# Another set of seven-product weight groups in a two-layer decoder trunk, with an accumulating transfer for one weight sum and the query and key squares summed on ScalarE

## The chip, the cores and the metric

The program runs on one core of one Trainium2 chip. The metric is the device time of one execution, in microseconds (us); the kernel before takes 1815.41 us (median of 3 runs, 1814.85 to 1815.59). The engines are named as in the profile: PE is TensorE, DVE VectorE, ACT ScalarE, POOL GpSimd and SP SyncE. On this chip each engine works through its own instructions in order; an instruction that waits holds up all that stand behind it on the same engine. PEld are PE's loads of a stationary operand, which run beside its matmuls.

## What is computed

Two layers are applied to x of 512 tokens by 2048 features. Each normalises x, projects it with one weight matrix, runs three mixers on slices of the projection, gates each, and projects the 2048 mixed features back into the residual:

```python
def _layer(x, norm_g, w_in, conv_w, conv_b, sb_qn_g, sb_kn_g, gla_w_up, gla_b_up, gla_on_g, w_out):
    h = _rmsnorm(x, norm_g)
    proj = h @ w_in                                   # 2048 x 7696
    (cv_h, cv_b, cv_c, cv_g, sb_q, sb_k, sb_v, sb_g, gl_q, gl_k, gl_v, gl_g, gl_lr) = split(proj)
    y_conv = _short_conv(cv_h, cv_b, cv_c, conv_w, conv_b) * silu(cv_g)
    q, k = _rmsnorm(sb_q, sb_qn_g), _rmsnorm(sb_k, sb_kn_g)      # 8 heads of 128
    y_sb = _stick_breaking(q, k, sb_v) * silu(sb_g)
    g = log_sigmoid(gl_lr @ gla_w_up + gla_b_up) / 16
    o = _gla(gl_q, gl_k, gl_v, g)                     # 4 heads, keys of 64, values of 128, decayed
    y_gla = _rmsnorm(o, gla_on_g) * silu(gl_g)
    return x + concat(y_conv, y_sb, y_gla) @ w_out
```

## The kernel before

**Weight groups.** The weights are worked through in groups of 256 columns by 2048 rows, 38 a layer, always in the order of the list `specs`: two value groups of the gated linear attention (GLA), its query, its key, its two gates, four groups of the first half of the convolution (h, c, g, b), then for each of four pairs of heads of the attention v, g, q, k (v 0, g 0, q 0, k 0, v 1, ...), the four groups of the second half of the convolution, and eight groups of the output projection. `fetch` loads a group's 2 MB on SP's queue two groups ahead, into one of two buffers `st`. `load_` prepares it one group ahead: `wmax` (ACT, squares with their sum), an all-reduce on POOL and a few instructions on 128x1 columns on DVE (`wscale`) give a power of two, and the scaled weights are split into two f16 parts, the high one by ACT and the low one by DVE. The inputs are split in the same way, so that a product takes three f16 matmuls (high by high, high by low, low by high).

**Plain and seven-product groups.** A plain group is split in two halves (lines L432 on ACT, L439 on DVE) and multiplied by 16 k-tiles in `project_cols` (features on the partitions, 96 matmuls of 512 columns) or `project_toks` (tokens on the partitions, 192 of 256 columns). A group named in `QUICK_IN` or `QUICK` is taken as a 2x2 block matrix and multiplied with seven block products instead of eight, by a scheme of the Strassen kind (`project_quick`: 168 matmuls of 256 columns, or 336 of 128). Before it, `wsums` forms sums of the four weight blocks b11, b12, b21, b22 with four DVE additions in place in `st` and splits seven blocks (L471 on ACT, L472 on DVE) into seven operands; after it, DVE and ACT combine the products. The products also need four sums of the blocks of the input: the first, fifth and seventh product read the input alone, the second and sixth read one of the four sums each, and so do the third and the fourth. `xsums` makes them once a layer: 24 additions of 128x1024 on DVE (one line, L673) and 8 copies on ACT (L681). Its scratch tiles come from the tags `zw` and `g`, of which there are two buffers each.

**What sets the order.** Beyond a part at the very start that is ordered by hand, a scheduler places the instructions of every engine when the program is built, by dependencies, by free buffers and by its own estimate of the times; the order on each engine is then fixed. Code written later comes later in it only where dependencies, priorities or buffers make it so. The weights' preparation has a higher priority. The squares of the next group are issued after the instruction in `lasthi`.

**Around the change.** `xsums()` is called ahead of the GLA's query. The GLA works on two pairs of heads (p = 0, 1). For each, seven levels of block products are built (L998 to L1012: differences on DVE, Exp on ACT, splits on ACT and DVE, `mm3` on PE, a masked copy into the tile `attd`, of the tag `zw`, on DVE), then four inter-chunk products (L1059, L1060), then the products with the values (L1072). The tail of each pair, for each of two heads, scales the result (L1078), squares it on ACT, means it on PE (L1082), takes Ln and Exp on ACT, and runs six DVE instructions of 128x512 (L1086 to L1091). In the attention, v is split (L1241, L1242) and its largest size found by DVE and an all-reduce (L1243, L179); queries and keys are squared by ACT in two halves of 128x512 (L1271), summed by DVE in groups of 128 (L1272), normalised, split, transposed by DMA and used for scores (L1181) a group or two later.

## Time and profile before

| | |
|---|---|
| median of 3 runs | 1815.41 us |
| the profiled execution | 1812.69 us, of which the span is 1810.9 us |
| mean granted clock of PE | 0.973 |
| PE, PEld busy | 1687.5 us (93%), 1384.3 us (76%) |
| DVE busy | 1447.8 us (80%) |
| ACT busy | 1149.2 us (63%) |
| POOL busy | 75.7 us (4%) |
| stretch from the GLA's query to the attention's first query, layer 1 and 2 | 269.2 us, 270.4 us |
| stretch of the attention and the second convolution half, layer 1 and 2 | 409.8 us, 408.2 us |
| output projections | 162.8 us, 161.2 us |

A row of a group of instructions reads: line, engine, operation, tile written <- tiles read, shape, count, then busy time in us and mean ns of one, then the engine's idle time ahead of these instructions and what ended it. A row of a table of windows gives a stretch (start and end in us from the start of the span), its length, and each engine's busy time in it with the number of instructions; PEclk is the granted clock of PE. Busy times of matmuls hold their drain, so the distance between two starts is less than a matmul's duration.

### The profile page before, as it was taken

The numbers are of one execution on the slowest core, as the hardware profiler recorded it, in microseconds if no ns is written. First come the engines' busy times: TensorE is split into PE (matmuls) and PEld (weight loads), VectorE is DVE, ScalarE is ACT, GpSimd is POOL, SyncE is SP. The second block draws the span as 40 slices with busy tenths as digits, with TensorE's granted clock in tenths as the row PEclk, the third lists the DMA queues.
The fourth block names the chain that finished last, engine by engine and source line by source line (L and its number), as shares of the span: only waits on it lengthen the run. The fifth ranks groups of instructions, "written<-read, shape, count | busy, mean of one in ns | idle before, by whom it ended". The sixth has DMA issues, their size and how long they took to land. (4 is left out here: it accounts for less than half of the span.)

```text
span 1810.9 us, 37130 instructions
## 1 busy us (share of the span) xinstructions
PE 1687.5 (93%) x15786; PEld 1384.3 (76%) x15786; DVE 1447.8 (80%) x2539; ACT 1149.2 (63%) x1459; POOL 75.7 (4%) x106
## 2 busy tenths in 40 slices
PE   8997979889998999999999878889899989999999
PEld 6656756778887885689986666568888888847998
DVE  8989997768687786777598899976687868767884
ACT  7568766746574665656666686755575657655562
POOL 1100000000000000000011000000000000000000
PEclk9998989999999999999999999999999999999999
DMA  6221222333554447344643112314253635562541
GB/s 238 94 93 48 94 90 69 115 114 109 143 127 121 113 128 217 108 147 151 213 117 125 48 52 95 99 59 152 71 169 83 175 77 160 163 189 76 180 143 48
DMA packets 297926, 217.83 MB, mean 120 GB/s; under 512 B 118482, under 2 KB 296988, under 8 KB 297248
## 3 DMA queue, kind: packets, MB, share of 16 engines
q1 hardware_dynamic: 288752, 206.01, 38.2%
q10 hardware_dynamic: 9008, 9.45, 1.5%
q8 instruction: 123, 2.02, 0.4%
q14 instruction: 43, 0.35, 0.1%
HBM read 179.65 MB, written 14.68 MB: 107 GB/s over the span
## 5 line engine op out<-in xcount | busy, mean ns | idle before, releaser
L653 PE MATMUL psp<-wh,m 128*128 128x256 f16 x1088 | 296.4, 273 | 2.9 <-DVE v L1242 1.8
L655 PE MATMUL psp<-wh,m 128*128 128x256 f16 x1088 | 296.5, 273 | 0.0
L654 PE MATMUL psp<-wl,m 128*128 128x256 f16 x1088 | 296.5, 273 | 0.0
L472 DVE SCALAR_TENSOR_TENSOR wl<-st,ws,wh 128x1024 f16<-128x1024 f32 x186 | 235.0, 1279 | 71.4 <-ACT wh L471 71.1
L365 ACT ACTIVATE junk<-st 128x2048 uint8<-128x2048 f32 x150 | 285.0, 1900 | 4.4 <-DMA st<-in_w_out_dram 2.9
L471 ACT ACTIVATE wh<-st,ws 128x1024 f16<-128x1024 f32 x186 | 205.8, 1140 | 88.6 <-PE psp L655 33.5
L732 PE MATMUL psp<-s,wh 128*128 128x256 f16 x1280 | 229.8, 280 | 27.5 <-ACT wh L471 8.2
L439 DVE SCALAR_TENSOR_TENSOR wl<-st,ws,wh 128x2048 f16<-128x2048 f32 x90 | 211.1, 2348 | 54.2 <-ACT wh L432 53.6
L432 ACT ACTIVATE wh<-st,ws 128x2048 f16<-128x2048 f32 x88 | 175.5, 1998 | 93.3 <-DVE wp L395 31.2
L732 PEld LDWEIGHTS <-wh 128*128 128x128 f16 x1920 | 193.2, 101 | 47.4 <-ACT wh L471 15.5
L732 PE MATMUL psp<-s,wl 128*128 128x256 f16 x640 | 178.8, 280 | 4.9 <-DVE wl L472 4.3
L653 PE MATMUL psp<-wh,x 128*128 128x256 f16 x640 | 174.3, 273 | 2.9 <-DVE v L1242 1.9
L654 PE MATMUL psp<-wl,x 128*128 128x256 f16 x640 | 174.4, 273 | 0.0
L655 PE MATMUL psp<-wh,x 128*128 128x256 f16 x640 | 174.4, 273 | 0.0
L732 PEld LDWEIGHTS <-wl 128*128 128x128 f16 x960 | 96.6, 101 | 59.8 <-issue 26.9
L654 PEld LDWEIGHTS <-m 128*128 128x128 f16 x1088 | 106.5, 98 | 14.6 <-issue 2.4
L653 PEld LDWEIGHTS <-m 128*128 128x128 f16 x1088 | 106.5, 98 | 13.2 <-issue 0.6
L655 PEld LDWEIGHTS <-m 128*128 128x128 f16 x1088 | 106.5, 98 | 12.5 <-issue 0.2
L378 POOL PARTITION_ALL_REDUCE wgm<-wm x75 | 46.1, 615 | 1537.1 <-ACT junk L365 1316.0
L779 PEld LDWEIGHTS <-m 128*128 128x128 f16 x768 | 74.8, 98 | 13.5 <-DMA m<-raw 3.1
L645 PE MATMUL psp<-x,wh 128*128 128x512 f16 x192 | 74.0, 385 | 9.8 <-ACT wh L432 9.8
L645 PEld LDWEIGHTS <-wh 128*128 128x128 f16 x384 | 37.9, 99 | 56.0 <-ACT wh L432 12.5
(426 smaller groups left out, 3833.6 us busy)
## 6 DMA issues: line engine op xcount, KB each, us to landing
st<-in_w_in_dram SPq DMA_DIRECT2D x120, 1024.0 KB, 7.6
st<-in_w_out_dram SPq DMA_DIRECT2D x32, 1024.0 KB, 6.7
mixd<-ga SPq DMA_DIRECT2D x24, 256.0 KB, 2.6
x<-in_x_dram SPq DMA_DIRECT2D x4, 1024.0 KB, 4.9
qT<-in_x_dram ACTq DMA_DIRECT2D x8, 512.0 KB, 4.7
qT<-xs ACTq DMA_DIRECT2D x8, 512.0 KB, 3.8
xs<-x SPq DMA_DIRECT2D x14, 256.0 KB, 4.8
out_dram<-kT SPq DMA_DIRECT2D x14, 256.0 KB, 2.8
```

Source lines behind the costliest of these rows:

```text
L365: S.activation(junk(HK * GW).rearrange("p (k n) -> p k n", k=HK), staged[i][h], AF.Square, accum_out=peak[i][:, h:h + 1])
L378: G.partition_all_reduce(gm, peak.pop(i), P, RED.add)
L432: lasthi[i] = S.activation(wh[:, :, :GW], staged[i][h], AF.Copy, scale=scales[i])
L439: V.scalar_tensor_tensor(wl[:, :, :GW], staged[i][h], scales[i], wh[:, :, :GW], ALU.mult, ALU.subtract)
L471: hi = S.activation(h_, b, AF.Copy, scale=sc)
L472: V.scalar_tensor_tensor(l_, b, sc, h_, ALU.mult, ALU.subtract)
L645: T.matmul(o, wh[:, kk, cs], xh[:, :, k, :], start=st_, stop=False)
L653: T.matmul(o, ah[:, t, k, :], wh[:, kk, :n], start=st_, stop=False, skip_group_check=True)
L654: T.matmul(o, ah[:, t, k, :], wl[:, kk, :n], start=False, stop=False, skip_group_check=True)
L655: T.matmul(o, al[:, t, k, :], wh[:, kk, :n], start=False, stop=en, skip_group_check=True)
L732: T.matmul(o, w[q_][:, kk, :], a[p_][:, :, kk, :], start=st_, stop=en, skip_group_check=True)
L779: T.matmul(o[:, :n], a_[:, t, k, :], w[k // HK][part][:, k % HK, :n], start=i == 0 and k == 0, stop=i == 2 and k == KT - 1)
```

## The change

The set of seven-product input groups is another one: of each layer's input groups the nine g 0, k 0, g 1, k 1, g 2, k 2, g 3, k 3 and conv h 1 are now taken with seven products, and the GLA's gates, the first convolution half's h, c, g and the attention's v 1 and v 3 are plain. The output groups stay as they are.

In `wsums` the first sum, b12 + b11, is made by a DMA that POOL issues and that adds to its destination; the other sums are written so that three additions on DVE are left, and the order of the splits is another. The next group's squares are now tied to the first high part (`anchor`). In `wscale` one 128x1 instruction of DVE goes. `xsums()` is called after `conv_out(0, ...)`, which stands behind the whole GLA. The GLA's o_ is scaled by ACT. The bound of the attention's values no longer looks at v: the largest-size search on DVE and its all-reduce are gone. The squares of queries and keys are made and summed by ACT in eight pieces of 128x128, each with an accumulator.

```diff
-QUICK_IN = ("gla gate 0", "gla gate 1", "conv h 0", "conv c 0", "conv g 0", "v 1", "g 0", "g 1", "g 2", "v 3", "g 3",
-            "conv h 1")
+QUICK_IN = ("g 0", "k 0", "g 1", "k 1", "g 2", "k 2", "g 3", "k 3", "conv h 1")
...
-        p2 = sm(1, "wp")
-        V.tensor_scalar(p2.bitcast(I32), m.bitcast(I32), 0.5, float((50 + lift) << 23), ALU.mult, ALU.add)
         u = sm(1, "wu", bufs=6)
-        V.tensor_tensor(u, p2, mixun[l] if src is w_out else xun[:, l:l + 1], ALU.mult)
+        V.tensor_scalar(u.bitcast(I32), m.bitcast(I32), (outoff[l] if src is w_out else inoff)[lift][:, l:l + 1],
+                        None, ALU.add)
...
-        with tc.issue_after(lasthi[i - 1].ins):
+        with tc.issue_after(anchor[i - 1].ins):
             for h in range(2):
                 wmax(i, h)
...
+        G.dma_start(out=b12, in_=b11, accum_op=ALU.add)
         split(b11, 0)
-        V.tensor_tensor(b11, b11, b12, ALU.add)
-        split(b22, 3)
-        V.tensor_tensor(b12, b12, b22, ALU.add)
-        V.tensor_tensor(b22, b11, b22, ALU.add)
+        anchor[i] = split(b22, 3)
+        V.tensor_tensor(b22, b12, b22, ALU.add)
         split(b22, 1)
-        lasthi[i] = split(b12, 2)
-        V.tensor_tensor(b22, b22, b21, ALU.add)
+        V.tensor_tensor(b11, b22, b11, ALU.subtract)
+        split(b11, 2)
         split(b21, 4)
-        split(b11, 5)
-        split(b22, 6)
+        V.tensor_tensor(b21, b22, b21, ALU.add)
+        split(b12, 5)
+        split(b21, 6)
...
-        insums = xsums()
         scr = [wk([P, 2, 2, seq], *a, F16) for a in (("qp", 1), ("th", 2), ("th", 2))]
...
                 o_ = wk([P, seq], "za")
-                V.tensor_scalar(o_, ops_, gu[:, p:p + 1], None, ALU.mult)
+                S.activation(o_, ops_, AF.Copy, scale=gu[:, p:p + 1])
...
         conv_out(0, conv_in(0))
+        insums = xsums()
...
-            V.tensor_reduce(bm[:, 0:1], vh, AX.XY, ALU.max, apply_absolute_value=True)
...
             g, _ = project_gate(bm[:, 1:2], True)
-            gm = allmax(bm[:, 0:1], 1, "b")
...
                     e = wk([P, 2 * GW], "e")
-                    S.activation(e, rb.rearrange("p a c -> p (a c)"), AF.Square)
-                    V.tensor_reduce(sq[:, 4 * b:4 * b + 4], e.rearrange("p (a c) -> p a c", c=P), AX.X, ALU.add)
+                    for i in range(4):
+                        cs = slice(i * P, (i + 1) * P)
+                        S.activation(e[:, cs], rb.rearrange("p a c -> p (a c)")[:, cs], AF.Square,
+                                     accum_out=sq[:, 4 * b + i:4 * b + i + 1])
```

The lines of the changed kernel stand 4 to 8 further down (L673 is L677 there, L1091 is L1094, L732 is L736).

The first place is DVE and the additions of `xsums`. Before, in the first layer, they begin among the work of the first GLA value group (s_988 is one of the sums, wgm and wq belong to a weight group's scale):

```order
L673 TENSOR_TENSOR g_992<-x_180,x_181 128x1024
L380 TENSOR_TENSOR wgm_359<-wgm_359 128x1
L673 TENSOR_TENSOR zw_990<-x_180,g_992 128x1024
L381 TENSOR_SCALAR wq_358<-wgm_359 128x1
L673 TENSOR_TENSOR zw_990<-zw_990,x_181 128x1024
```

Now they stand behind the tail of the GLA's second pair of heads (za_2252 is its second head's result, ga_2655 belongs to the gate of the first convolution half):

```order
L1093 TENSOR_TENSOR za_2252<-za_2252,e_2258 128x512
L1094 SCALAR_TENSOR_TENSOR za_2252<-za_2252,par,g_1553 128x512
L677 TENSOR_TENSOR g_2816<-x_184,x_185 128x1024
L844 SCALAR_TENSOR_TENSOR ga_2267<-za_2252,gsmix_1577,ga_2267 128x512
L677 TENSOR_TENSOR zw_2814<-x_184,g_2816 128x1024
L677 TENSOR_TENSOR zw_2814<-zw_2814,x_185 128x1024
L677 TENSOR_TENSOR zw_2815<-x_184,zw_2814 128x1024
L677 TENSOR_TENSOR zw_2815<-zw_2815,x_185 128x1024
L677 TENSOR_TENSOR s_2812<-zw_2814,s_2812 128x1024
L813 SCALAR_TENSOR_TENSOR ga_2655<-g_2653,ga_2655 128x512
```

All 24 additions moved from the two GLA value groups to a place behind the last instruction of the GLA's tail, and the gate of the first convolution half is mixed in between them.

The second place is PE at the start of g 0, the first group behind the GLA that reads the sums. In the changed kernel the first product (psp_3124) is followed by the second (psp_3125, which reads s_2812) and the third (which reads s_2813):

```order
L736 LDWEIGHTS wh_2870
L736 MATMUL psp_3124<-x_185,wh_2870 128x256
...
L736 MATMUL psp_3125<-s_2812,wh_2870 128x256
L736 LDWEIGHTS wl_2871
L736 MATMUL psp_3125<-s_2812,wl_2871 128x256
L736 LDWEIGHTS wh_2872
L736 MATMUL psp_3124<-s_2813,wh_2872 128x256
```

Before, the products of the same group stand in this order (s_989 was written during the second GLA value group):

```order
L732 MATMUL psp_3637<-x_181,wh_3380 128x256
L732 LDWEIGHTS wh_3382
L732 MATMUL psp_3637<-s_989,wh_3382 128x256
L732 LDWEIGHTS wl_3383
L732 MATMUL psp_3637<-s_989,wl_3383 128x256
```

The order of the products is much the same; what moved is the work that writes their operands, which now stands late on DVE.

The third place is POOL, whose order in the attention is now a row of all-reduces (L382) with an adding transfer (L480) behind that of every seven-product group (st_2672 is g 0, st_3099 is k 0):

```order
L382 ISA wgm_2862<-wm_2856 128x2
L480 DMA st_2672<-st_2672 128x8x128
L382 ISA wgm_3108<-wm_3102 128x2
L382 ISA wgm_3326<-wm_3320 128x2
L480 DMA st_3099<-st_3099 128x8x128
L382 ISA wgm_3603<-wm_3597 128x2
```

Before, the same stretch holds all-reduces alone (L179 is that of the largest value):

```order
L378 ISA wgm_3619<-wm_3613 128x2
L179 ISA bgm_3822<-bm_3360 128x1
L378 ISA wgm_3841<-wm_3835 128x2
```

A transfer of 512 KB came in behind the all-reduce of each of the 25 seven-product groups, and the eight L179 went.

More of the change, by code (lines that the diff above doesn't have):

```diff
@@ L1258, in dst @@
                 def dst():
-                    raw.append(wk([P, NT, GW], "raw", 1))
+                    raw.append(wk([P, NT, GW], *(("raw", 1) if gain is None else ("kT",))))
                     return raw[0]
@@ L1263, in hybrid_trunk @@
                 copied = bool(raw)
-                raw = raw[0] if copied else dst()
+                if not copied:
+                    raw.append(wk([P, NT, GW], "raw", 1))
+                raw = raw[0]
                 sq = sm(8, "qs")
```

26 lines of the change are left out of this document (18 added, 8 removed).

## The prediction

> **What bounds the kernel now.** I read the shares of busy time first, then a table of windows by stage, cut where the first matmul of a weight group starts. Its columns are the stretch, its length, then busy time and instruction count of each engine.
>
> ```profile
> PE 1687.5 (93%) x15786; PEld 1384.3 (76%) x15786; DVE 1447.8 (80%) x2539; ACT 1149.2 (63%) x1459; POOL 75.7 (4%) x106
> ```
>
> ```profile
> 18.10:75.70 57.60, 53.90 (x437) 44.89 (x437) 55.84 (x112) 40.95 (x53) 6.78 (x5) 0.94 0.37 117
> 75.70:344.90 269.20, 231.71 (x1810) 170.43 (x1809) 239.64 (x451) 186.97 (x279) 11.45 (x15) 0.94 0.27 85
> 344.90:754.70 409.80, 394.99 (x3603) 326.35 (x3602) 306.32 (x555) 253.95 (x284) 11.86 (x22) 0.98 0.47 131
> 754.70:917.50 162.80, 161.48 (x1972) 150.32 (x1970) 122.60 (x167) 102.88 (x151) 6.47 (x10) 1.00 0.51 163
> 917.50:967.60 50.10, 47.08 (x419) 40.84 (x417) 47.08 (x72) 30.91 (x39) 5.47 (x4) 1.00 0.41 109
> 967.60:1238.00 270.40, 231.42 (x1809) 169.36 (x1807) 237.69 (x443) 187.11 (x280) 11.91 (x15) 0.94 0.27 84
> 1238.00:1646.20 408.20, 396.08 (x3602) 325.58 (x3600) 305.88 (x553) 251.90 (x280) 11.86 (x22) 0.98 0.47 131
> ```
>
> The output projection (754.7 to 917.5) is bound by PE: 161.5 of 162.8 us. So is the attention, with 14.8 and 12.1 us of idle PE (409.8 less 395.0, 408.2 less 396.1). The GLA stretch (75.7 to 344.9, and 967.6 to 1238.0) is not: PE idles 37 to 39 us in each layer. Inside it DVE is full:
>
> ```profile
> 138.90:166.20 27.30, 22.88 (x217) 19.83 (x215) 26.71 (x50) 23.52 (x38) 1.06 (x1) 0.94 0.24 78
> 166.20:197.60 31.40, 25.51 (x224) 21.08 (x222) 31.21 (x60) 27.34 (x50) 1.08 (x1) 0.89 0.18 58
> 241.90:286.70 44.80, 42.54 (x314) 27.22 (x315) 42.37 (x90) 32.96 (x60) 0.47 (x1) 0.90 0.25 80
> ```
>
> So a change pays in the attention by what it takes from PE, and in the GLA by what it does to the chain through DVE.
>
> **PE's price of a group.** Windows that hold one kind of group alone give it (PE's busy time and count, then the clock):
>
> ```profile
> 967.60:988.50 20.90, 20.90 (x102) 1.00 0.30 100
> 344.90:365.90 21.00, 21.00 (x195) 1.00 0.54 176
> 506.10:515.60 9.50, 9.50 (x87) 1.00 0.28 82
> 877.70:896.50 18.80, 18.80 (x338) 1.00 0.61 195
> ```
>
> A plain column group takes 20.9 us, a plain token group 21.0, a seven-product token group 18.8. The third row is 87 matmuls of a seven-product column group: 0.109 us each, so 168 take 18.3. A column group made plain costs 2.6, a token group made quick saves 2.2.
>
> **DVE's and ACT's prices.** Rows by line (busy, mean ns):
>
> ```profile
> L472 DVE SCALAR_TENSOR_TENSOR wl<-st,ws,wh 128x1024 f16<-128x1024 f32 x186 | 235.0, 1279 | 71.4 <-ACT wh L471 71.1
> L439 DVE SCALAR_TENSOR_TENSOR wl<-st,ws,wh 128x2048 f16<-128x2048 f32 x90 | 211.1, 2348 | 54.2 <-ACT wh L432 53.6
> L477 DVE TENSOR_TENSOR st<-st 128x1024 f32<-128x1024 f32 x31 | 37.8, 1220 | 0.3
> L754 DVE TENSOR_TENSOR g<-psp,g 128x256 f32<-128x256 f32 x21 | 8.8, 421 | 0.4
> L1272 DVE TENSOR_REDUCE qs<-e 128x4 f32<-128x512 f32 x32 | 21.7, 677 | 0.0
> L1271 ACT ACTIVATE e<-raw 128x512 f32<-128x512 f32 x32 | 20.2, 630 | 1.0
> L1042 ACT ACTIVATE e<-raw 128x128 f32<-128x128 f32 x12 | 3.5, 293 | 0.0
> L1325 ACT ACTIVATION_READ_ACCUMULATOR junk<-x 128x1 f32 x32 | 6.0, 186 | 0.0
> L471 ACT ACTIVATE wh<-st,ws 128x1024 f16<-128x1024 f32 x186 | 205.8, 1140 | 88.6 <-PE psp L655 33.5 <-PE psp L735 24.8 <-PE psp L732 11.6
> ```
>
> A seven-product group costs DVE 7 splits of 1.28, 4 sums of 1.22 and 5 combinations of 0.42, 15.9 us, a plain one 2 of 2.35, 4.7. The sum handed to the transfer saves 1.22.
>
> **The change, part by part. (1) The GLA stretch.** Five column groups turn plain: PE +13 us, DVE 5 times -11.2 = -56. With DVE relieved PE would set the pace; but the input sums now come behind the GLA. They used to lie in the two value groups:
>
> ```profile
> 18.10:75.70 57.60, 21.59 (x18) 0.94 0.37 117
> 917.50:967.60 50.10, 21.50 (x18) 1.00 0.41 109
> ```
>
> That is DVE on L673 alone: 18 of 24 sums, 1.20 us each; the other 6 follow at the start of the GLA stretch, long before any product reads them. In the new order they follow the last L1094 of the second pair of heads, since their scratch tiles are those of the GLA, and PE, which takes its instructions in order, comes to g 0's second product before they are done. The time up to g 0's end is walked in two pieces, cut at the second pair's last L1060. The GLA's end before, on DVE (start, duration):
>
> ```profile
> 291.56 0.68 DVE L1060 SCALAR_TENSOR_TENSOR za<-psz,za 128x512 f16<-128x512 f32 x1
> ...
> 293.89 0.68 DVE L1060 SCALAR_TENSOR_TENSOR za<-psz,za 128x512 f16<-128x512 f32 x1
> ...
> 302.99 0.69 DVE L1086 TENSOR_TENSOR e<-e 128x512 f32<-128x512 f32 x1 [4.54 <-ACT e L1085]
> ...
> 306.83 0.75 DVE L1091 SCALAR_TENSOR_TENSOR za<-za,par,g 128x512 f32<-128x512 f32 x1
> ...
> 318.35 0.74 DVE L1091 SCALAR_TENSOR_TENSOR za<-za,par,g 128x512 f32<-128x512 f32 x1
> ```
>
> Front piece, before: 294.6 - 75.7 = 218.9 us. After: PE must do 8 column groups (167.2), half of v 0 (10.5), and the GLA's own matmuls. Those are 231.7 less the groups before (3 x 20.9 + 6 x 18.3 + 21.0 = 193.5), 38.2, so 19 for the first pair and about 10 for the second up to this point: 207 us. DVE, behind the second pair's first block product, has some 30 us of instructions by the rows above; PE reaches that product after 721 of the 768 column matmuls (157) and the first pair (19), at 176, so DVE ends at 206 to 210. I take 209: **-10 us**.
>
> Tail piece, before: 344.9 - 294.6 = 50.3. After: the first L1086 comes 8.4 us behind the last L1060 (302.99 - 294.57). From there the order has, up to the last lo part that the second product reads, two tails of six instructions (3.9 each: 302.99 to 307.58 less one other), 5 splits (6.4), 17 of the sums (20.7), 8 instructions of the convolution and its gate (6.7, at 0.68 to 1.22), and 4.2 of small ones and single splits, 45.8 in all; consecutive starts lie some 0.06 closer than durations, 47 times: 43. Seven more sums and the convolution's splits until the fourth product's operand: 10.6. Then four products of 2.6. In all 8.4 + 43 + 10.6 + 10.5 = 72.5, **+22**. On ACT the order now has a weight split and two squares of 1.9 around the Ln of the first head: 0 to +4.7, taken as 3. So +15 us a layer, **+30**. PE then stands still for some 30 us at g 0's second product; DVE is what it waits for.
>
> **(2) The attention.** k 0 to k 3 turn quick (-8.8), v 1 and v 3 plain (+4.4): -4.4 a layer. PE's idle time there is at v 1 with g 1 and v 3 with g 3, two seven-product groups in a row (waits of PE from 386 to 460):
>
> ```profile
> PE psp L735 <- ACT kT L743: 4.4, 1, 4.4
> PE psp L732 <- ACT wh L471: 1.2, 1, 1.2
> PE psp L732 <- DVE wl L472: 1.0, 1, 1.0
> ```
>
> With the two of 0.5 that this answer also lists, 7.6 us a pair; where a plain group stands between, as from 483.5 to 571, PE has none. After the change only k 3 and conv h 1 meet: one pair a layer is left, -7.4 and about -6. Together -11.8 and -10.4: **-22**. The squares give ACT 8 x (0.293 + 0.186) - 2 x 0.63 = +2.6 us a group and take 1.35 from DVE; 8 groups put 21 us on ACT in a stretch where it is busy 254 of 410. The k chain gets under 1 us longer and has v's 21 us of PE work as its cover; without it the scores wait by that much. Cost nothing. So do the value's search (DVE, -1.2 a pair, POOL) and the 128x1 instruction: PE covers them.
>
> **(3) The value groups at a layer's start** lose 22 us of DVE, which is busy 55.8 of 57.6 and 47.1 of 50.1; PE idles 3.7 and 3.0 there. Between 0 and -6.7, mostly waits for weights and x: **-2**.
>
> **(4) The adding transfer**, 25 of 512 KB. No row shows one; the nearest:
>
> ```profile
> st<-in_w_in_dram SPq DMA_DIRECT2D x120, 1024.0 KB, 7.6
> mixd<-ga SPq DMA_DIRECT2D x24, 256.0 KB, 2.6
> qT<-in_x_dram ACTq DMA_DIRECT2D x8, 512.0 KB, 4.7
> ```
>
> From 2.6 us to 15.2 (twice the weights' 7.6, as it reads both operands and writes one). I take 7, the 4.7 of the row of its size and half as much again. The Trainium skill, page "DMA: Bandwidth & Descriptors", section "Anatomy of one DMA — SWDGE (gpsimd) path", gives about 2.0 us and bytes over 436 GB/s for a transfer that POOL issues: an estimate of 3.2 us by that page, under which this term is nothing too; no run here shows it yet. Its cover: the group's scale, two splits on ACT and DVE in turn (at least 4.5 us by the rows) and in the attention other DVE work, near 9. So 0 at 7, and a loss from 9 on. The output groups keep 18.8 us of PE: 0.
>
> **The sum**, against the profiled execution of 1812.7 (span 1810.9): +30 - 22 - 2 = +6, 1818.7. The median of the runs is 2.7 higher: **1821 us**.
>
> **Rivals.**
> *A, faster:* the sums cost less than I walk, since the front piece gains more. DVE's load in the stretch falls to 240 - 56 + 22 = 206 us and PE's is 245 (206.5 of groups and 38.2), so with a third of its present waits the stretch would take 257 and the kernel 1767. For it: DVE was full there. Against: the sums stand behind the chain's end in DVE's order, and PE can do nothing else. It decides where the stretch grows by less than 10 us a layer; at no growth the time is 1821 - 30 = 1791, which I take for A.
> *B, the transfer is late:* at 12 us DVE stands 3 us in each of 25 groups; where PE has no slack all 75 count, 1896, and at half of it 1858. For it: fetches of 1 MB run at the same time. Against: it starts right behind the all-reduce.
> *C, no relief in the attention:* ACT's added 21 us and the even spread of quick groups put as much idle time back: 1843.
>
> **How the numbers follow.** My forecast (1812 to 1833, by 10 to 20 us a layer in the GLA) gets 0.50, A 0.27, B 0.15, C 0.08. No change is within 0.2%, 3.6 us, about what a measurement tells: 0.13, the forecast's lower edge. Faster: A and a little, 0.29. Slower: 0.58. The range leaves out A's deeper part (0.1) and B's upper half (0.08): 1793 to 1858.
>
> **What would show it.** Right: PE waits of 25 to 35 us a layer in front of g 0's second product, released by the sums (L677, or their high parts, L685); the GLA stretch near 284 us; the attention near 398; the transfer landing in under 9 us, with no wait of L483 for a DMA. Wrong: a GLA stretch under 279 us, or waits for the transfer's queue on DVE.

## The result, and the profile after

The changed kernel takes 1813.01 us (median of 12 runs, 1810.41 to 1819.41), the kernel before 1815.57 us (median of 12 on the same chip, 1811.57 to 1817.97): a ratio of 0.9993, with a 95% interval of 0.9981 to 1.0004. That is no change that can be measured, within the 0.2% that the prediction set for it, and 8 us below the forecast of 1821 (range 1793 to 1858). The profiled execution of the changed kernel was the slowest of its twelve, 1819.41 us with a span of 1817.3, so the two profiles stand 6.4 us of span apart where the medians stand 2.6 us apart the other way. The stages below are those of the two profiles.

The first part of the page of the changed kernel, shares of busy time:

```profile
PE 1681.9 (93%) x15642; PEld 1307.9 (72%) x15642; DVE 1331.5 (73%) x2312; ACT 1138.9 (63%) x1627; POOL 94.7 (5%) x123
```

DVE lost 116 us of work and PE 6, and the time stood still. The table of windows by stage of the changed kernel (GLA, attention and output projection of layer 1, GLA and attention of layer 2):

```profile
74.40:355.60 281.20, 237.27 (x1459) 134.46 (x1458) 207.91 (x367) 171.49 (x248) 8.20 (x14) 0.92 0.30 86
355.60:746.70 391.10, 384.40 (x3877) 320.39 (x3875) 298.24 (x536) 266.82 (x401) 20.38 (x26) 1.00 0.62 146
746.70:919.00 172.30, 164.41 (x1971) 153.08 (x1969) 119.03 (x152) 102.38 (x150) 10.69 (x13) 0.97 0.58 162
...
969.10:1249.30 280.20, 236.89 (x1460) 134.16 (x1458) 208.00 (x367) 171.41 (x248) 7.98 (x14) 0.92 0.30 87
1249.30:1642.20 392.90, 384.55 (x3875) 320.19 (x3874) 298.05 (x536) 266.53 (x398) 21.09 (x26) 1.00 0.63 145
```

Three stages moved, and they cancel. Against the kernel before, by the same cuts (layer 1, layer 2); the cut between GLA and attention lies about 0.2 us later in all these kernels than in the prediction's rows, so before has 269.4 here for 269.2 there:

| stage | before | after | difference, both layers | forecast |
|---|---|---|---|---|
| value groups | 57.6, 50.1 | 54.5, 50.1 | -3.1 | -2 |
| GLA stretch | 269.4, 270.6 | 281.2, 280.2 | +21.4 | +30 |
| attention | 409.6, 408.0 | 391.1, 392.9 | -33.6 | -22 |
| output projection | 162.8, 161.2 | 172.3, 171.4 | +19.7 | 0 |

With 1.8 us that the first value group starts later (19.9 for 18.1) that is +6.2 of the two spans' 6.4.

**The GLA stretch** ends on the input sums. The waits of PE around its end (line waited for, total, times, longest), first layer 1 and then layer 2:

```profile
PE psp L736 <- ACT s L685: 34.2, 2, 33.6
PE psm L1085 <- ACT e L1083: 7.1, 1, 7.1
```

```profile
PE psp L736 <- ACT s L685: 33.6, 2, 32.9
```

PE stands 33 us a layer at g 0's second product, released by the high part of a sum. The timeline of DVE in layer 1 (start, duration) gives the pieces:

```profile
273.85 0.69 DVE L1063 SCALAR_TENSOR_TENSOR za<-psz,za 128x512 f16<-128x512 f32 x1 [0.67 <-ACT za L1062]
...
288.66 0.69 DVE L1089 TENSOR_TENSOR e<-e 128x512 f32<-128x512 f32 x1
...
304.36 0.75 DVE L1094 SCALAR_TENSOR_TENSOR za<-za,par,g 128x512 f32<-128x512 f32 x1
...
305.15 1.22 DVE L677 TENSOR_TENSOR g<-x,x 128x1024 f32<-128x1024 f16 x1
...
340.80 1.22 DVE L677 TENSOR_TENSOR s<-zw,s 128x1024 f16<-128x1024 f32 x1
```

The last instruction of the front piece (now L1063) ends at 274.5, 200.1 us after the stretch's start; before it was 218.9. From there to g 0's end it is 81.1 us, before 50.5. The 24 sums lie between 305 and 342.

**The output projection** lost its even run on PE. Waits of PE in it, layer 1, DVE's two longest waits for the transfer in a timeline of the same stretch, and the page's row of the transfer:

```profile
PE psp L739 <- DVE g L758: 4.7, 1, 4.7
PE psp L739 <- DVE wl L476: 2.5, 1, 2.5
```

```profile
806.60 1.22 DVE L483 TENSOR_TENSOR st<-st 128x1024 f32<-128x1024 f32 x1 [2.70 <-DMA st<-st]
...
831.45 1.23 DVE L483 TENSOR_TENSOR st<-st 128x1024 f32<-128x1024 f32 x1 [5.18 <-DMA st<-st]
```

```profile
st<-st POOLq DMA_DIRECT2D x25, 512.0 KB, 9.0
```

DVE waits for the adding transfer, and the seven-product groups of the projection wait for what stands behind that on DVE: their splits and the combinations of the group ahead. PE's idle time in the stage went from 1.3 to 7.9 us (172.3 less 164.4), and its clock from 1.00 to 0.97. Before, PE's waits in the same stage were these two:

```profile
PE psp L735 <- ACT g L750: 0.9, 1, 0.9
PE psp L735 <- ACT g L743: 0.4, 1, 0.4
```

### The profile page after: what moved, and what is told of

Same layout as the page of the kernel before. It is cut to its first block, busy times and chain, and to the rows that moved or that the text cites. A ratio compares the mean times of both kernels' runs of the same rounds, so it can differ in the third digit from the quotient of the medians.

```text
span 1817.3 us, 36858 instructions
## 1 busy us (share of the span) xinstructions
PE 1681.9 (93%) x15642; PEld 1307.9 (72%) x15642; DVE 1331.5 (73%) x2312; ACT 1138.9 (63%) x1627; POOL 94.7 (5%) x123
## 5 line engine op out<-in xcount | busy, mean ns | idle before, releaser
L659 PE MATMUL psp<-wh,m 128*128 128x256 f16 x960 | 261.8, 273 | 0.0
L657 PE MATMUL psp<-wh,m 128*128 128x256 f16 x960 | 261.7, 273 | 0.0
L476 DVE SCALAR_TENSOR_TENSOR wl<-st,ws,wh 128x1024 f16<-128x1024 f32 x150 | 189.4, 1278 | 80.7 <-ACT wh L475 80.6
L475 ACT ACTIVATE wh<-st,ws 128x1024 f16<-128x1024 f32 x150 | 166.1, 1140 | 86.1 <-PE psp L659 50.2
L736 PE MATMUL psp<-s,wh 128*128 128x256 f16 x640 | 112.7, 279 | 69.1 <-ACT s L685 67.8
L657 PE MATMUL psp<-wh,x 128*128 128x256 f16 x512 | 140.1, 274 | 0.0
L659 PE MATMUL psp<-wh,x 128*128 128x256 f16 x512 | 140.0, 273 | 0.0
L651 PE MATMUL psp<-x,wl 128*128 128x512 f16 x352 | 133.4, 379 | 0.0
L651 PE MATMUL psp<-m,wl 128*128 128x512 f16 x352 | 133.4, 379 | 0.0
L650 PE MATMUL psp<-x,wh 128*128 128x512 f16 x352 | 133.4, 379 | 0.0
L650 PE MATMUL psp<-m,wh 128*128 128x512 f16 x352 | 133.4, 379 | 0.0
L649 PE MATMUL psp<-m,wh 128*128 128x512 f16 x352 | 133.2, 379 | 0.0
L649 PE MATMUL psp<-x,wh 128*128 128x512 f16 x352 | 133.2, 379 | 0.0
L650 PEld LDWEIGHTS <-wh 128*128 128x128 f16 x704 | 68.8, 98 | 81.7 <-issue 1.1
L649 PEld LDWEIGHTS <-wh 128*128 128x128 f16 x704 | 68.8, 98 | 80.7 <-issue 0.5
L382 POOL PARTITION_ALL_REDUCE wgm<-wm x75 | 38.2, 509 | 1558.2 <-ACT junk L369 1395.0
```

Source lines behind the costliest of these rows:

```text
L475: hi = S.activation(h_, b, AF.Copy, scale=sc)
L476: V.scalar_tensor_tensor(l_, b, sc, h_, ALU.mult, ALU.subtract)
L649: T.matmul(o, wh[:, kk, cs], xh[:, :, k, :], start=st_, stop=False)
L650: T.matmul(o, wh[:, kk, cs], xl[:, :, k, :], start=False, stop=False)
L651: T.matmul(o, wl[:, kk, cs], xh[:, :, k, :], start=False, stop=en)
L657: T.matmul(o, ah[:, t, k, :], wh[:, kk, :n], start=st_, stop=False, skip_group_check=True)
```

## The experiments

Twelve kernels were run, each beside the kernel before, whose median there was 1816.7 to 1818.8 us. They are compared by their ratios to it; a difference of ratios is turned into us with 1817. Their stages, in us, layer 1 and layer 2, by the same cuts:

| | ratio, 95% interval | GLA stretch | attention | output projection |
|---|---|---|---|---|
| before | 1 | 269.4, 270.6 | 409.6, 408.0 | 162.8, 161.2 |
| after | 0.9993, 0.9981 to 1.0004 | 281.2, 280.2 | 391.1, 392.9 | 172.3, 171.4 |
| sums_early | 0.9725, 0.9708 to 0.9743 | 260.0, 252.1 | 393.7, 394.3 | 173.1, 171.6 |
| add_on_dve | 0.9867, 0.9852 to 0.9882 | 280.5, 280.0 | 387.6, 387.5 | 161.1, 165.4 |
| early_dve | 0.9607, 0.9592 to 0.9621 | 260.1, 255.2 | 388.2, 391.0 | 161.0, 165.2 |
| squares_dve | 1.0000, 0.9988 to 1.0012 | 280.0, 280.0 | 390.6, 392.8 | 173.1, 169.3 |
| early_out_dve | 0.9657, 0.9638 to 0.9675 | 258.6, 255.2 | 394.1, 394.8 | 161.1, 165.4 |
| half_transfer | 0.9901, 0.9883 to 0.9920 | 281.5, 280.6 | 391.8, 387.7 | 162.7, 164.3 |
| old_set | 1.0054, 1.0037 to 1.0070 | 276.5, 273.8 | 401.9, 405.0 | 172.7, 168.5 |
| set_alone | 0.9809, 0.9792 to 0.9825 | 247.6, 246.5 | 416.1, 415.8 | 162.8, 163.6 |
| set_order | 0.9865, 0.9849 to 0.9882 | 258.3, 255.5 | 409.8, 411.7 | 161.1, 164.1 |
| set_search | 0.9750, 0.9735 to 0.9764 | 246.7, 245.3 | 411.9, 409.1 | 162.8, 164.5 |
| early_dve_o | 0.9631, 0.9614 to 0.9649 | 259.2, 255.0 | 393.5, 388.4 | 161.0, 165.0 |
| early_dve_anchor | 0.9592, 0.9576 to 0.9608 | 253.9, 252.2 | 394.6, 394.1 | 161.0, 159.0 |

### The sums in their old place (sums_early)

The changed kernel with the call of `xsums` put back ahead of the GLA:

```diff
+        insums = xsums()
         scr = [wk([P, 2, 2, seq], *a, F16) for a in (("qp", 1), ("th", 2), ("th", 2))]
...
         conv_out(0, conv_in(0))
-        insums = xsums()
```

> The changed kernel with the input sums (24 additions, 8 copies) back ahead of the GLA's query; nothing else differs from it. Theory (the sums are late): the 34 us that PE waits in front of g 0's second product in each layer go, the front piece of the GLA stretch stays near its 210 us and the tail falls back to 50 to 54, so a stretch takes 260 to 265 us instead of 280 and the kernel 1813 - 2 x 17 = 1779 us (1768 to 1788). Rival (DVE is the bound wherever the sums lie): the value groups at a layer's start grow by 3 us or more and the stretch only falls to about 275; 1798 to 1811 us.

1770.5 us, inside the theory's range and 48.7 us less than the changed kernel (0.9993 less 0.9725, of 1817). The GLA stretch falls by 21 and 28 us, and PE has no wait for the sums left. The late sums are the cause of the growth; they cost 21 and 28 us; with the sums in their old place the stretch is 9 and 18 us shorter than before.

### The transfer's addition back on DVE (add_on_dve)

```diff
-        G.dma_start(out=b12, in_=b11, accum_op=ALU.add)
         split(b11, 0)
+        V.tensor_tensor(b12, b12, b11, ALU.add)
         anchor[i] = split(b22, 3)
```

> The changed kernel with the first weight sum of all 25 seven-product groups as an addition on DVE instead of the adding transfer. Theory (the transfer takes 9 us and is late where two seven-product groups of the output projection follow each other): the output projections fall from 172 and 171 us to about 163 and 162, the attention stays within 3 us (1.2 us more on DVE a group, hidden), the GLA stretch is the same; in all 10 to 20 us faster than the changed kernel, 1793 to 1803 us. Rival (the output groups wait because of the new order of the splits, not for the transfer): the output projections stay at 170 us or more; 1810 to 1818 us.

1795.6 us, 22.9 us less than the changed kernel and inside the theory's range. The output projection is back at 161.1 us in layer 1; in layer 2 it comes to 165.4, 6.0 us less than in the changed kernel and still 4.2 more than before. The attention gains 3.5 and 5.4 us, and the GLA stretch, whose end the sums set, does not move. Here 25 additions of 1.22 us on DVE are cheaper than the transfers that replace them.

### Both together (early_dve)

Both edits above.

> Both of the above: sums ahead of the GLA and the first weight sum on DVE. Theory: the two gains stand in different stages and add up, 1779 - 17 = 1762 us (1750 to 1775). Rival: with the sums early DVE is the bound in the GLA stretch, and the additional sum there or the loss of slack in the attention takes half of it back; 1775 to 1790 us.

1748.4 us, a ratio of 0.9607: faster than both kernels, and 1.6 us below the theory's range. The two costs simply add: 48.7 and 22.9 are 71.6, the measured difference to the changed kernel is 70.1 (0.9993 less 0.9607). Waits of PE in its attention of layer 1, all that there are:

```profile
PE psp L736 <- ACT g L754: 3.7, 3, 1.5
PE psp L739 <- ACT kT L754: 0.5, 1, 0.5
```

### The query and key squares summed by DVE (squares_dve)

```diff
-                    for i in range(4):
-                        cs = slice(i * P, (i + 1) * P)
-                        S.activation(e[:, cs], rb.rearrange("p a c -> p (a c)")[:, cs], AF.Square,
-                                     accum_out=sq[:, 4 * b + i:4 * b + i + 1])
+                    S.activation(e, rb.rearrange("p a c -> p (a c)"), AF.Square)
+                    V.tensor_reduce(sq[:, 4 * b:4 * b + 4], e.rearrange("p (a c) -> p a c", c=P), AX.X, ALU.add)
```

> The changed kernel with the query and key squares as before: two squares of 128x512 on ACT and two sums on DVE a group. Theory (hidden either way in the attention): within 4 us of the changed kernel, 1809 to 1817 us, attention 390 to 395 us. Rival (the attention's gain comes from the 10.8 us a layer that leave DVE): attention 5 to 10 us longer in each layer, 1823 to 1833 us.

1818.3 us, a ratio of 1.0000 beside 0.9993 with overlapping intervals, and the attention at 390.6 and 392.8. With the rest of the change in place, this edit is worth nothing that can be measured in either direction: hidden either way, as the theory said.

### The transfer in the input groups alone (early_out_dve)

early_dve with the transfer put back where the weights are not those of the output projection:

```diff
+        if specs[i][1] is not w_out:
+            G.dma_start(out=b12, in_=b11, accum_op=ALU.add)
         split(b11, 0)
-        V.tensor_tensor(b12, b12, b11, ALU.add)
+        if specs[i][1] is w_out:
+            V.tensor_tensor(b12, b12, b11, ALU.add)
```

> The version with the sums early, where the first weight sum of the seven output groups is an addition on DVE and that of the 18 input groups stays with the adding transfer. Theory (two places of harm: in the output projection the transfer is late, in the attention it costs some 4 us a layer): output projections 161 and 165 us, attention 393 to 394, in all 1770 - 18 = 1752 us (1748 to 1757). Rival (the transfers cost the same everywhere): half of the 22 us between the two versions comes back, 1757 to 1763 us.

1753.9 us. The output projection has the times of early_dve, the attention 394.1 and 394.8 us for 388.2 and 391.0. By the ratios the transfers of the 18 input groups cost 9.1 us (0.9657 less 0.9607) and those of the seven output groups 12.4 (0.9725 of sums_early less 0.9657; 18 by the stages of the two profiles). How much of the input groups' cost lies in the attention is less certain than its 4 to 6 us a layer suggest: early_dve_o below, which has no transfer either, takes 393.5 us there in layer 1.

### Half the transfer (half_transfer)

The changed kernel, with half of the sum added by the transfer (256 KB) and half by DVE:

```diff
-        G.dma_start(out=b12, in_=b11, accum_op=ALU.add)
+        q = HK // 2
+        G.dma_start(out=b12[:, :q], in_=b11[:, :q], accum_op=ALU.add)
         split(b11, 0)
+        V.tensor_tensor(b12[:, q:], b12[:, q:], b11[:, q:], ALU.add)
```

> The changed kernel with half of the first weight sum (256 KB) by the adding transfer and the other half on DVE. Theory (the transfer's time grows with its size: 6.5 us alone, 9 to 13 beside others, for 512 KB): it lands in 4 to 6 us, the output projections fall to 164 to 166 us, and the kernel takes 1794 to 1802 us. Rival (its fixed part decides): it lands in 6 us or more as before, the output projections stay near 170, 1804 to 1813 us.

1798.2 us, inside the theory's range and 16.7 us less than the changed kernel; the output projection (162.7 and 164.3) is 9.6 and 7.1 us shorter. The page's row of the smaller transfer:

```profile
st<-st POOLq DMA_DIRECT2D x25, 256.0 KB, 5.2
```

In the output groups of both layers the smaller transfers land 4.2 to 6.6 us behind their issue, those of the changed kernel 6.4 to 11.4, and DVE has no wait for a transfer left in the projection of layer 1. So it is not by itself that POOL issues a transfer which costs there, but that it lands late. The shorter transfer is not the only reason for landing earlier: in the projection of layer 1 POOL issues it 1.9 to 2.8 us ahead of the group's all-reduce, where the changed kernel issues it 0.6 to 0.8 us behind the start of that; the two were not run apart.

### The old set in the changed kernel (old_set)

sums_early with the twelve groups of before:

```diff
-QUICK_IN = ("g 0", "k 0", "g 1", "k 1", "g 2", "k 2", "g 3", "k 3", "conv h 1")
+QUICK_IN = ("gla gate 0", "gla gate 1", "conv h 0", "conv c 0", "conv g 0", "v 1", "g 0", "g 1", "g 2", "v 3", "g 3",
+            "conv h 1")
```

> The changed kernel with the set of seven-product groups of before and the sums ahead of the GLA: transfers, squares on ACT, o_ on ACT and no value search stay. Theory (the transfer fits only where a plain group stands ahead; the old set has five seven-product groups in a row and two pairs): its lateness shows in the GLA stretch, 275 to 300 us, and in the output projections, 170 to 173, so 1835 to 1880 us. Rival (DVE is full in that stretch, and the addition taken from it outweighs the wait): the stretch falls under 268 us and the kernel takes 1805 to 1820 us.

1826.4 us, 10 us slower than before and 60 us slower than sums_early (1.0054 less 0.9725). Theory and rival both missed, and the theory's reason does not show, since DVE waits for a transfer in the output projections alone. Inside the new code the set of nine is worth 60 us, by the stages 17 and 22 us in the GLA stretch and 8 and 11 in the attention.

### The set alone (set_alone)

The kernel before with the new set and nothing else:

```diff
-QUICK_IN = ("gla gate 0", "gla gate 1", "conv h 0", "conv c 0", "conv g 0", "v 1", "g 0", "g 1", "g 2", "v 3", "g 3",
-            "conv h 1")
+QUICK_IN = ("g 0", "k 0", "g 1", "k 1", "g 2", "k 2", "g 3", "k 3", "conv h 1")
```

> The kernel before with the new set of seven-product groups and nothing else: sums ahead of the GLA, four weight sums on DVE, squares summed by DVE, the largest-size search on v kept. Theory (the set is the gain; squares, value search and sum on other engines are hidden): attention 390 to 394 us instead of 409, GLA stretch 257 to 262 instead of 270, output projections as before, 162 and 161; in all 1816 - 33 - 20 = 1763 us (1750 to 1775), within 15 us of the version with the sums early and no transfer. Rival (the attention only gains because DVE is relieved of its sums and searches): attention above 400 us and 1780 us or more.

1782.4 us, 34.7 us less than before and in the rival's range. The GLA stretch gains 22 and 24 us. The attention, where a gain was expected, gets 6.5 and 7.8 us longer. The table of windows of this kernel in the attention, and PE's waits there:

```profile
323.30:739.40 416.10, 395.62 (x3889) 326.63 (x3888) 324.18 (x584) 259.68 (x293) 13.14 (x22) 0.97 0.46 130
```

```profile
PE psp L653 <- DVE wl L438: 8.6, 3, 3.8
PE psp L652 <- ACT wh L431: 3.6, 3, 2.1
PE psp L734 <- ACT raw L742: 2.9, 1, 2.9
PE psp L731 <- DVE wl L471: 2.8, 1, 2.8
PE psm L1217 <- DVE e L1224: 2.5, 2, 2.0
```

The waits at v 1 with g 1 and v 3 with g 3 are gone, and three of another kind stand in their place: at the plain v 1, v 2 and v 3, each of which PE now takes up in the middle of a seven-product key group, for the splits of their own weights. PE is idle 20.5 us (416.1 less 395.6) where it was 14.8 before.

### The set with the new order of the weight sums (set_order)

set_alone with the new order of sums and splits and the earlier hold for the next group's squares, all four additions on DVE:

```diff
-        lasthi[i] = S.activation(wh[:, :, :GW], staged[i][h], AF.Copy, scale=scales[i])
+        hi = S.activation(wh[:, :, :GW], staged[i][h], AF.Copy, scale=scales[i])
+        lasthi.setdefault(i, hi)
...
-        V.tensor_tensor(b11, b11, b12, ALU.add)
-        split(b22, 3)
-        V.tensor_tensor(b12, b12, b22, ALU.add)
-        V.tensor_tensor(b22, b11, b22, ALU.add)
+        V.tensor_tensor(b12, b12, b11, ALU.add)
+        lasthi[i] = split(b22, 3)
+        V.tensor_tensor(b22, b12, b22, ALU.add)
...
-        lasthi[i] = split(b12, 2)
-        V.tensor_tensor(b22, b22, b21, ALU.add)
+        V.tensor_tensor(b11, b22, b11, ALU.subtract)
+        split(b11, 2)
...
-        split(b11, 5)
-        split(b22, 6)
+        V.tensor_tensor(b21, b22, b21, ALU.add)
+        split(b12, 5)
+        split(b21, 6)
```

> The set alone with the new order of weight sums and splits (all on DVE) and the next group's squares tied to the first high part; value search, squares and the sums' place as before. Theory (k 0 to k 3 stall in the set alone because their last operands and the next group's squares come late in the old order): attention from 416 to 392 to 398 us, the kernel from 1782 to 1745 us (1738 to 1755). Rival (DVE's relief by the value search and the squares makes the difference): attention stays above 408 us, 1768 us or more.

1791.7 us, in the rival's range and 10.2 us slower than the set alone. The attention comes to 409.8 and 411.7 us, 4 to 6 less than with the set alone and 21 to 22 more than in early_dve, and the GLA stretch is 9 to 11 us a layer longer. The order is not by itself what relieves the attention: the waits for v's splits stay, 12.1 us in layer 1 where the set alone has 12.2.

```profile
PE psp L654 <- DVE wl L439: 7.3, 3, 2.6
PE psp L653 <- ACT wh L431: 4.8, 3, 2.6
```

### The set without the search for v's largest size (set_search)

set_alone with:

```diff
-            V.tensor_reduce(bm[:, 0:1], vh, AX.XY, ALU.max, apply_absolute_value=True)
...
-            V.tensor_scalar(vu[:, 0:1], u, 2.0 ** 14, None, ALU.mult)
+            V.tensor_scalar(vu[:, 0:1], u, 2.0 ** 29, None, ALU.mult)
...
-            gm = allmax(bm[:, 0:1], 1, "b")
...
-            V.scalar_tensor_tensor(m, gm, vu[:, 0:1], bm[:, 1:2], ALU.mult, ALU.mult)
-            s_ = mixscale(2 + j, m, "b")
+            V.tensor_tensor(m, vu[:, 0:1], bm[:, 1:2], ALU.mult)
+            s_ = mixscale(2 + j, m, "b", 12.0)
```

> The set alone without the largest-size search over v (no maximum on DVE, no all-reduce on POOL; the bound is twice that of before). Theory (the order of the weight sums is what matters): attention stays at 412 to 416 us, 1776 to 1784 us. Rival (the search and its all-reduce hold up the chain to the values and block POOL and DVE ahead of the next scale): attention falls to 395 to 402 us, 1745 to 1758 us.

1770.9 us, 10.7 us less than the set alone, 4 to 7 us a layer of it in the attention (411.9, 409.1). Both theories missed, and this alone does not bring the attention to 390 either. The waits for v's splits in layer 1 are those of the set alone again:

```profile
PE psp L653 <- DVE wl L438: 8.9, 3, 3.6
PE psp L652 <- ACT wh L431: 3.1, 3, 2.1
```

### o_ scaled by DVE (early_dve_o)

```diff
-                S.activation(o_, ops_, AF.Copy, scale=gu[:, p:p + 1])
+                V.tensor_scalar(o_, ops_, gu[:, p:p + 1], None, ALU.mult)
```

> The version with the sums early and the first weight sum on DVE, and the GLA's o_ scaled by DVE again, as before. Theory (o_ on ACT puts the square and with it PE's mean behind ACT's weight splits: PE waits 7.0 us for that square in each layer there, 0.7 us in the set alone): the GLA stretch falls from 260 and 255 to about 250 us, the kernel from 1748 to 1733 us (1726 to 1740). Rival (the wait only passes to the split of v on DVE, for which the set alone waits 9 us): the stretch stays within 3 us, 1743 to 1752 us.

Put into early_dve: 1748.9 us, 0.9631, and a GLA stretch of 259.2 and 255.0. That is early_dve within the measurement, as the rival said; the place of this instruction explains nothing of the difference between 260 and 247 us.

### The later hold for the next group's squares (early_dve_anchor)

early_dve, with the squares of the next group tied to the last high part of a plain group and to the fourth in order of a seven-product group:

```diff
-        anchor.setdefault(i, hi)
+        anchor[i] = hi
...
-        anchor[i] = split(b22, 3)
+        split(b22, 3)
...
-        split(b11, 2)
+        anchor[i] = split(b11, 2)
```

> The version with the sums in their old place and DVE adding (1748.4 us), but the load of the next group's weights held behind the group's last high part on ACT, as before the change, and no longer behind an earlier one. Theory: the earlier hold puts the next group's squares between the Ln and the Exp of the GLA's last heads on ACT, and costs the 7 us that PE waits at the mean of their squares; the GLA stretch falls from 260 and 255 to 247 to 250 a layer, the attention stays at 388 to 391, 1724 to 1738 us. Rival: the attention's gain needs the earlier hold; the GLA falls alike, the attention goes back to 405 or more, and the kernel takes 1760 us or more.

1744.6 us, a ratio of 0.9592: the fastest, though not by more than the intervals overlap. Both theories missed. The GLA stretch falls by 6 and 3 us to 253.9 and 252.2, not to 247 to 250; the attention goes up by as much, not to 405; and the wait at the mean of the squares, which the earlier hold was to have made, is still there (PE's waits of layer 1 from 60 to 330 us, the three longest):

```profile
PE psm L1086 <- ACT e L1084: 8.1, 1, 8.1
PE psp L736 <- ACT g L747: 3.9, 1, 3.9
PE psp L736 <- ACT g L751: 2.8, 1, 2.8
```

What the later hold is worth by the profiles lies where neither theory looked, in the output projection of layer 2, first of early_dve and then of early_dve_anchor, which has no wait of PE left there:

```profile
1578.30:1743.50 165.20, 160.16 (x2115) 150.32 (x2112) 118.49 (x141) 77.07 (x80) 5.72 (x6) 1.00 0.38 122
1579.40:1738.40 159.00, 159.00 (x2115) 150.04 (x2112) 118.25 (x143) 79.74 (x81) 12.98 (x7) 1.00 0.40 126
```

The GLA stretch is still 6 to 7 us longer than that of set_search, and the timelines show a part of what differs. In set_search, whose stretch takes 246.7 us, the store of the first of the last two heads (L841 on SP's queue) is issued at 288.8. On ACT the first step of the convolution's gate (L805) and g 0's second combination (L746) then stand at:

```profile
302.78 0.61 ACT L805 ACTIVATE ga<-g 128x512 f32<-128x512 f32 x1
...
307.53 0.37 ACT L746 ACTIVATE g<-psp 128x256 f32<-128x256 f32 x1
```

In early_dve_anchor both heads' stores come from 300.35 on (one row on SP's queue), and the same two steps of ACT stand at:

```profile
309.25 0.63 ACT L810 ACTIVATE ga<-g 128x512 f32<-128x512 f32 x1 [4.19 <-DMA mixd<-ga]
...
311.63 0.36 ACT L751 ACTIVATE g<-psp 128x256 f32<-128x256 f32 x1
```

The gate writes a buffer of `ga` that the stores read, waits 4.2 us for one of them, and g 0's combination, on which PE waits, stands behind the gate. Every kernel here with both the new set and the new order of weight sums has this wait, 3.8 to 4.8 us in each layer, early_dve and set_order among them. set_alone and set_search, with the old order, have none, and neither has old_set, with the new order and the old set. So it goes with the new order under the new set and not with the hold; that it accounts for the 7 us between 253.9 and 246.7 is read from the rows, and no run took it away alone.

## Why the prediction was right, and which of its reasons were not

The result lies in the range, at the lower edge of the forecast (1812 to 1833). That the sum came out is luck. The table of stages has the GLA stretch 8.6 us under its term, the attention 11.6 us under, and the output projection 19.7 us over a term of nothing: three errors that cancel. The agreement of the profiled executions (+6.7 for a forecast of +6.0) is partly luck too, since that of the changed kernel was the slowest of its twelve; by the medians nothing got slower.

Of the signs that the prediction named, the wait at g 0's second product and the GLA stretch came as said. The attention came out shorter than its 398 us, the transfer lands in 9.0 us in the median and not under 9, and a sign of being wrong is there: DVE waits for the transfer at L483 four times, 11.0 us in all, each time in an output projection.

The runs take the change apart along one line, each step being the difference of two ratios:

| step | us |
|---|---|
| before to set_alone: the set | -34.7 |
| set_alone to early_dve: order of sums and earlier hold, search, squares, o_, the 128x1 instruction | -36.7 |
| early_dve to add_on_dve: the sums behind the GLA | +47.2 |
| add_on_dve to after: the transfer | +22.9 |

**Step (1), the GLA stretch: right in its mechanism, its two pieces too small.** PE waits 33 us a layer at g 0's second product for a sum's high part, as said (25 to 35, L677 or L685), and the stretch measured 281.2 and 280.2 for a forecast of near 284. The front piece gained 18.8 us, not 10; the tail piece lost 30.6, not 25. Of the 5.6 us by which the tail (81.1) exceeds its walk (72.5 and 3), 2.7 lie before the first L1089, which comes 14.1 us behind the front piece and not 11.4 (8.4 and the 3 for ACT). The cold clock behind the wait is in no term of the walk: the table of windows of the changed kernel, right behind it,

```profile
334.80:338.00 3.20, 1.87 (x8) 1.01 (x8) 3.20 (x6) 1.66 (x2) 0.00 (x0) 0.50 0.00 0
338.00:341.00 3.00, 3.00 (x19) 2.18 (x18) 3.00 (x5) 1.79 (x3) 0.00 (x0) 0.61 0.00 0
341.00:345.00 4.00, 4.00 (x39) 3.57 (x38) 2.95 (x3) 3.64 (x2) 0.00 (x0) 1.00 0.51 131
```

shows 19 matmuls in 3 us where the next 4 us hold 39. Rival A, that the relief of DVE shows in full, holds where the sums stay in their place, and by more: set_alone's 247 us is 10 below the 257 that it gave. In the changed kernel A fails at the place that the prediction named against it, the sums behind the chain's end in DVE's order.

**Step (2), the attention: right in its sign, too small, and for another reason.** The prediction gave -11.8 and -10.4 us a layer to four key groups made quick and to the neighbours v with g that part; measured are -18.5 and -15.1. But set_alone, which does just that, makes the attention 7 us a layer longer. The waits were not removed by the set, they moved to the plain v groups beside the quick key groups. What failed is the count of pairs as the whole of the term, and the sentence that the value's search costs nothing since PE covers it; the new order of sums has no price at all. The search alone gives 4 to 7 us, the order alone 4 to 6; with both and one further relief of DVE per group, be it the transfer (squares_dve, 390.6 and 392.8) or the squares on ACT (early_dve, 388.2 and 391.0), the attention falls by 23 to 28 us against the set alone. Both kernels lack the 128x1 instruction besides, and have o_ on ACT, which is not needed for it (early_dve_o, 393.5 and 388.4); whether search and order without a further relief would do was not run. The squares alone are hidden as costed, with the transfer in place.

How these edits work together is not that each shortens the wait for v's splits: set_alone, set_order and set_search all have about 12 us of it in layer 1. What differs is the order in which PE works. Here are PE's matmuls of k 0 (L734 in set_alone, L739 in early_dve, each alone) from the end of q 0 up to the first matmul of v 1, first in set_alone and then in early_dve:

```profile
344.10:351.60 7.50, 5.49 (x96) 1.00 0.09 14
354.50:370.60 16.10, 16.06 (x288) 1.00 0.43 133
```

In set_alone PE turns to v 1 after 96 of the 336 matmuls of k 0 and waits there; in early_dve it first does 288, and v 1's splits are ready. set_order and set_search have the 96 of set_alone, and every kernel here with the new set and an attention under 400 us has 288 or all 336. So the scheduler gave PE another order once search and order of sums were both changed; which further edit that needs stays open.

The clock is part of it. By the rows of windows, layer 1 gains 18.7 us: 8.1 of idle time (14.8 to 6.7) and 10.6 of PE's busy time (395.0 to 384.4), of which the prediction's own prices of the groups make 4.4. 6.2 are left over. Its clock went from 0.98 to 1.00 in the rows of the two kernels, which of 395 us is 8, about as much within the rounding of such a figure. So here the waits seem to have cost more than their length; this is worked out from the rows, and no run isolates it.

**Step (3)** was within its small bounds: -3.1 for -2.

**Step (4), the adding transfer: the term failed for the output groups.** The prediction took 7 us and a loss from 9 on; the median is 9.0, inside the bounds of 2.6 to 15.2. Its sentence "the output groups keep 18.8 us of PE: 0" was wrong: there the stage got 9.5 and 10.2 us longer, and add_on_dve takes 11.2 and 6.0 of that back. The other 4 us of layer 2 are still in early_dve and gone in early_dve_anchor, so by these two profiles they go with the hold, which the prediction does not price. The sentence asked how long PE is busy with a group, and not whether DVE, which waits at the second sum for the transfer, is through the next group's splits by then; half_transfer, where that wait is gone, has the stage back at 162.7 us. In the attention, where the prediction named a cover near 9 us, DVE of the changed kernel never waits for a transfer, though the longest there takes 13.6 us; the stage is 3.5 and 5.4 us longer with the transfers, by what path no run shows. The mechanism is rival B's, at a third of its price (22.9 for 75 us). Four single transfers as windows, each from its issue to its landing (two of the output projection, one of the attention, one of the GLA); the last but one number is the share in which the DMA engines are busy:

```profile
820.30:831.40 11.10, 10.87 (x195) 10.69 (x192) 3.33 (x6) 3.74 (x5) 1.58 (x1) 1.00 0.98 235
865.80:872.20 6.40, 6.40 (x61) 5.75 (x59) 2.96 (x5) 2.30 (x2) 1.51 (x1) 1.00 0.76 93
567.90:581.50 13.60, 13.60 (x148) 12.42 (x146) 8.70 (x34) 3.94 (x16) 1.62 (x2) 1.00 1.17 216
1135.70:1142.10 6.40, 6.40 (x50) 3.60 (x48) 6.34 (x15) 4.45 (x7) 1.58 (x1) 1.00 0.73 82
```

The two that take 6.4 us have the DMA engines at 0.73 to 0.76 and 82 to 93 GB/s, the long ones at 0.98 and 1.17 and over 200 GB/s; that the load makes them long is read from these rows, and no run isolates it. The estimate that the prediction worked out from the Trainium skill, page "DMA: Bandwidth & Descriptors", section "Anatomy of one DMA — SWDGE (gpsimd) path", was 3.2 us; the trace differs, since the quickest of 25 took 6.4 and the slowest 13.6.

**Rival C**, that ACT's added work gives the relief back, was wrong: the attention gained more than forecast.

## What to carry to other kernels

An instruction on an engine with idle time is not free when something that PE waits for stands behind it in that engine's order: ask of each edit what it delays. Where a scheduler places the instructions, look also whether PE's own order has changed: in the attention the waits for v's splits went away with such a change, which no count of busy time shows. When work is moved out of a stage, look at which instruction now stands last in front of the next consumer; here 24 additions that cost little among the value groups cost 47 us behind the GLA. A change of several edits is best run one edit at a time: this one, which measured as nothing, held 71 us of gain and 70 us of loss, and undoing two of its edits gives 1748 us.

## What was unexpected of the hardware

An adding transfer of 512 KB between two places of `st` takes 6.4 us at its best, and up to 13.6 us where other transfers run beside it; half of it takes 4.2 us at its best and 10.4 at its worst.

The clock falls late. In early_dve_anchor PE waits 3.9 us in g 0, runs on at the full clock for 1.2 us and only then at half (the table of windows: wait, then two stretches behind it):

```profile
301.10:305.10 4.00, 0.13 (x2) 0.00 (x0) 3.07 (x6) 0.99 (x2) 0.00 (x0) 1.00 1.03 331
305.10:306.30 1.20, 1.18 (x11) 1.06 (x11) 0.48 (x1) 0.00 (x0) 0.00 (x0) 1.00 1.09 383
306.30:309.20 2.90, 2.90 (x15) 1.90 (x14) 0.00 (x0) 0.00 (x0) 0.00 (x0) 0.50 1.03 259
```

The slow matmuls stand 1.2 us away from the wait that belongs to them, so a wait of 3.9 us cost about 1.3 us more (15 matmuls in 2.9 us, which at the 11 in 1.2 of the row above would take 1.6). The Trainium skill, page "TensorE: Matmul & The Clock Gate", section "What's actually happening", has the clock set by PE's recent activity, with one idle window of about 3.4 us enough to halve it; this trace agrees with a wait of 3.9 us, and shows the lag besides.
